# A transformer block in split fp32 on one Trainium2 core: side work of the second span's projections placed elsewhere

## Chip, cores and metric

The kernel runs on one core of one Trainium2 chip. The metric is the device time of one execution in microseconds. The kernel before takes 2897.58 us (median of three runs, 2896.61 to 2900.97).

## What is computed

One layer over 2048 tokens of width 1024, all in fp32 (the reference, cut):

```python
xn = rms_norm(x, mix_norm_g)
proj = xn @ w_in                       # q k v | mq mk mv mo | i f | ga gm
A = chunk_band_attention(q, k, v)      # 8 heads of 64, own chunk of 64 and 8 before it
M = mlstm_chunkwise(conv_silu(mq), conv_silu(mk), mv, i, f)   # 4 heads of 128
M = sigmoid(mo) * headwise_rms_norm(M) * mh_norm_g
y = sigmoid(ga) * (A @ w_att_proj) + sigmoid(gm) * (M @ w_mlstm_proj)
x = x + y @ w_out
x = x + relu(rms_norm(x) @ w_up)**2 @ w_down      # 4096 wide
return rms_norm(x, final_norm_g)
```

## The kernel before

**Blocks and spans.** The tokens are four blocks of 512; blocks 0 and 1 are the first span, 2 and 3 the second ("far"). The first span's projections are plain products, block by block (`dense`, first loop). Everything behind them works on a span at once.

**Split products.** Each fp32 operand is split in two parts that TensorE takes at full rate (a rounded copy by ScalarE, the rest by VectorE: L420 and L422 for a weight tile, L953 and L958 or L955 and L960 for an operand tile). A product is three matmuls: high-high, high-low, low-high.

**Quads.** Most products of the spans use seven products of sums in place of eight (Strassen's scheme in Winograd's form). A quad (`quad`, L564) takes seven weight tiles and seven sets of four operand tiles and issues 7 x 2 x 4 x 3 = 168 matmuls of 512 columns. Its seven products share six banks of PSUM (`PLACES`): a product whose bank was used before waits until that bank was copied (L1742, on ScalarE) or added up (L1750, on VectorE; L1987 in the output projection). `combine` holds these two for all quads but the output projection. The operands' sums are made by `take_parts` (loads L1706, a gain L1709, sums L1719, splits) or by `spread` (L1804 to L1813); a set of five buffers holds them meanwhile.

**Sums of weights.** A quad's weight tiles are sums of four quarter tiles. Either `quad_w` makes them when the quad's turn comes (loads L397, VectorE L439) and, if the second span uses them again, stores them (L434); or `sum_w` makes them ahead (loads L384, VectorE L389, stores to `wsum`), and the loader later fetches seven finished tiles (L402). `sum_w` works in two halves; in each its fourth subtraction waits until the store of the first has landed, since it overwrites that buffer.

**Order of the work.** From 661 us on (all times by the profile of before) stand: two gate quads "gm" of the first span, two output quads (745), then the second span's projections in the order `IN_ORDER`: gm0, gm1, q, mq, vm0, ga0, k, vm1, mk, ga1, mo (mo at 1227); then eight up quads (from 1273), seven passes of the down projection (`down`, with `add_down`, L2187, adding up its banks), and the same from the output projection on for the second span (from 2184). In the first down projection run also attention and recurrence of blocks 2 and 3 (`attention_far`, `recurrence_far`; narrow matmuls L1210, L1245, L1276, L1586 to L1588), and inside it, at two fixed places, each of these blocks' mixer outputs are projected (`project`), for which their attention and recurrence must be done.

**Normalisation of the second span.** `norm_far` loads blocks 2 and 3 twice (L874, L897), squares them (L876), scales them (L899) and stores them as `xn`, from which `take_xn` makes the operands of `IN_ORDER`.

**Who sets the order.** The kernel is written as threads that a planner (`Flow`) runs when the program is built. Each thread asks for an engine with a duration; the planner keeps a clock for each engine, takes the request that can start first, and among those that could start at the same time the one with the lower rank, then the older. The order so found is the order of each engine's instructions in the program; on the chip each engine takes its own in that order and waits where data is late. The durations are the planner's own (`act_ns`, `dve_ns`, 0.67 us for the POOL operation in `after_in`, 2 us from a DMA's issue to its landing). All DMAs are issued by SP, in order, so that one that waits holds those behind it. Pools of buffers (16 `ctx`, 6 `tmp`) make a thread wait as well.

The lines that the prediction speaks of are these: L1742 and L1750 (`combine`), L1987 (`after_out`), L2187 (`add_down`), L1919 (the gate scale of mo, on POOL), L1941 (the convolution's activation, on ScalarE), L1706, L1709 and L1719 (`take_parts`), L389 (`sum_w`), L439 and L434 (`quad_w`).

Of the kernel before, what the change touches and what calls it, by code (L numbers as in the profile page):

```python
# [49 lines left out]
Q_VM, Q_IN = N_Q, dict(q=N_Q + 2, mq=N_Q + 3, ga0=N_Q + 4, k=N_Q + 5, mk=N_Q + 6, ga1=N_Q + 7, mo=N_Q + 8)  # L50
IN_ORDER = ("gm0", "gm1", "q", "mq", "vm0", "ga0", "k", "vm1", "mk", "ga1", "mo")
N_REC = 1
D_SUMS = (3, 6, 9, 11, 12, 13, 14, 15)
PROJ = {2: (4,0), 3: (6,2)}

ORDER = (0, 1, 3, 2, 5, 4, 6)
# [35 lines left out]
class Flow:  # L92
# [77 lines left out]
    def run(self):  # L170
        while self.ready or self.blocked:
            moved = True
            while moved:
                moved = False
                for th in sorted(self.blocked, key=lambda x: (x.prio, x.n)):
                    ok, value = self._grant(th)
                    if ok:
                        self.blocked.remove(th)
                        self.now = th.at
                        self._step(th, value)  # L180
                        moved = True
            if not self.ready and not self.blocked:
                break
            if not self.ready:
                raise RuntimeError("no thread can go on")
            best = None
            for th in self.ready:
                t, frm = th.at
                for e in th.req[0].split("|"):
                    start = t + self.LAT[frm].get(e, 0.0)  # L190
                    if e == "pe" and th.prio < 5:
                        start += self.SLACK
                    key = (max(self.clock[e], start), th.prio, th.n)
                    if best is None or key < best[0]:
                        best = (key, th, e)
            (start, _, _), th, e = best
            self.ready.remove(th)
            end = start + th.req[1]
            self.clock[e] = end
            if len(th.req) > 2:  # L200
                end += th.req[2]
            th.at = self.now = (end, e)
            self._step(th, e)
# [15 lines left out]
class Layer:  # L219
# [98 lines left out]
    def weights(self):  # L318


        part = lambda q, m: ("part", (q, m))
        for b in range(2):
            yield from (("plain", n) for n in range(N_W))
        yield from (part(q, m) for q in range(N_G + N_O) for m in range(7))
        for name in IN_ORDER:
            if name[:2] == "vm":
                yield from (part(Q_VM + kk, m) for m in range(7) for kk in range(2))
            elif name[:2] == "gm":
                yield from (part(int(name[2]), m) for m in range(7))
            else:  # L330
                yield "quad", (Q_IN[name], False)
        for s in range(NS):
            if s == 1:
                yield from (part(q, m) for q in range(N_G, N_G + N_O) for m in range(7))
            for q in range(N_G + N_O, N_G + N_O + N_F):
                if s == 0:
                    yield "quad", (q, True)
                else:
                    yield from (part(q, m) for m in range(7))
            for p, m in enumerate(ORDER):  # L340
                for q in range(N_Q - N_F, N_Q):
                    if s == 0 and (p, (q - N_Q + N_F) / 2) in PROJ.values():
                        yield from (("plain", N_W - 8 + 4 * x + j) for j in range(4) for x in range(2))
                    yield part(q, m)
# [280 lines left out]
    def dense(self):  # L625
        fl = self.fl
        none = [None] * KT
        for b in range(2):
            B = self.blk[b]
            self.banks.want = 4  # L630
            yield "wait", [B["xs_ev"]]
            fl.spawn(self.attention(b), 1)
            fl.spawn(self.recurrence(b), 1)
            xs = B["xs"]
            vs = xs if b > 0 else B["xg"]
            yield from self.token_tiles(vs, B["xn"], lambda t, bk: self.evac_v(b, t, bk))

            yield "wait", [self.ev_late]
            (bk,) = yield "get", self.banks, 1
            for k in range(KT):  # L640
                yield "pe", 433
                for j in range(2):
                    self.nc.tensor.matmul(bk[:40], self.gw[:, k], vs[k][:, j],
                                          start=k == 0 and j == 0, stop=k == KT - 1 and j == 1)
            fl.spawn(self.gates(b, bk), 1)
            yield from self.token_tiles(vs, none, lambda t, bk: self.evac_mv(b, t, bk))
            self.banks.want = 2
            if b == 0:
                fl.put(self.rpool, *vs)
            for j in range(4):  # L650
                for fn in (self.evac_q, self.evac_k, self.evac_conv_q, self.evac_conv_k, self.evac_og):
                    (bk,) = yield from self.feature_tile(xs, none if b > 0 or j > 0 else B["xs_done"])
                    fl.spawn(fn(b, j, bk), 1)
            if b == 0:
                fl.spawn(self.norm_in(1), 3)
                fl.spawn(self.norm_far(), 3)
            for j in range(8):
                (bk,) = yield from self.feature_tile(xs, none)
                fl.spawn(self.evac_ga(b, j, bk), 1)
            fl.put(self.rpool, *xs)  # L660
            fl.set(B["xs_free"])
            if b == 1:
                G = self.operands()
                for k in range(4):
                    fl.spawn(self.take_xn(0, k, *G), 2)
            early = range(N_G + N_O) if b == 0 else range(Q_VM, Q_VM + 2)
            for q in early:
                fl.spawn(self.sum_w(q), 3)
            self.banks.want = 3
            for x, evac in ((0, self.evac_att), (1, self.evac_rec)):  # L670
                for j in range(4):
                    yield "wait", B["mix_ev"][4 * x:4 * x + 4]
                    bks = yield from self.pair_tile(B["mix"][4 * x:4 * x + 4], none)
                    for n in range(2):
                        fl.spawn(evac(b, 2 * j + n, bks[n]), 1)
                fl.put(self.rpool, *B["mix"][4 * x:4 * x + 4])
# [11 lines left out]
            yield from self.quad(*O, self.after_out(0, i, None), release=i == N_O - 1)  # L688

        for i, name in enumerate(IN_ORDER):  # L690
            if i in D_SUMS:
                fl.spawn(self.sum_w(N_Q - N_F + D_SUMS.index(i)), 3)
            last = name == IN_ORDER[-1]
            if last:
                for k in range(4):
                    fl.spawn(self.take_x2(k, *U), 2)
            if i == 1:
                yield from self.gates_in(*X)
            if name[:2] == "vm":
                yield from self.quad_tok(int(name[2]), *X, self.after_vm(int(name[2])))  # L700
            else:
                yield from self.quad(*X, self.after_in(name), release=last)
        for s in range(NS):
# [4 lines left out]
                        fl.spawn(self.take(self.hd.ap(), self.h_ev, 1.0, (0, 1), *U), 2)  # L708
                    yield from self.quad(*O, self.after_out(1, i, U), release=i == N_O - 1)
            for i in range(N_F):  # L710
                if s == 0 and len(IN_ORDER) + i in D_SUMS:
                    fl.spawn(self.sum_w(N_Q - N_F + D_SUMS.index(len(IN_ORDER) + i)), 3)
                if i == 2:
                    for h in range(2):
                        fl.spawn(self.norm_mid(s, h), 3)
# [981 lines left out]
    def take_parts(self, src, kept, scale, k, A, aev, g=None):  # L1697
        fl, V = self.fl, self.nc.vector
        if k > 1:
            yield "wait", [aev[m][k - 2] for m in range(7)]  # L1700
        got = yield "get", self.ctx, 5
        a11, a12, a21, a22, s1 = (x[:, :512] for x in got)
        for b, j, a in ((0, k, a11), (0, 4 + k, a12), (1, k, a21), (1, 4 + k, a22)):
            yield "wait", [kept[b][j]]
# [15 lines left out]
            fl.spawn(self.take_split(dst, m, k, A, aev, scale), 1)  # L1720
            done.append(aev[m][k])
        yield "wait", done
        fl.put(self.ctx, *got)

    def take_split(self, src, m, k, A, aev, scale=1.0):
        (r,) = yield "get", self.rpool, 1
# [4 lines left out]
    def combine(self, finish, o=0):  # L1731
# [6 lines left out]
        def copied(n, name, ps, clear):  # L1738
            (t,) = yield "get", self.ctx, 1
            held[n][name] = t  # L1740
            yield "act", act_ns(512, True)
            nc.scalar.copy(t[:, o:o + 512], ps)  # L1742
            fl.set(clear)
            fl.set(ev[n][name])
# [1 line left out]
        def summed(n, name, to, ps, clear):  # L1746
            yield "wait", [ev[n][name]]
            t = held[n][name]
            yield "dve", dve_ns(512)
            nc.vector.tensor_add(t[:, o:o + 512], ps, t[:, o:o + 512])  # L1750
            if clear is None:
                fl.put(self.banks, ps)
# [146 lines left out]
    def after_in(self, name):  # L1899
        fl, nc = self.fl, self.nc  # L1900

        def finish(n, which, t, ps):
# [12 lines left out]
            if ps is not None:  # L1915
                fl.put(self.banks, ps)
            if name == "mo":
                yield "pool", 670
                nc.gpsimd.tensor_scalar(t5, t5, 1.0, self.ghead[:, j:j + 1], op0=ALU.add, op1=ALU.mult)  # L1919
                dst, ev = self.mfar[b].ap()[2 * MH + j], self.m_ev[b, 2 * MH + j]  # L1920
            else:
                x, j = name[:2] == "gm", 4 * hi + 2 * int(name[2]) + n
# [33 lines left out]
    def after_out(self, s, q, U):  # L1956
# [24 lines left out]
        def add(n, w, done, ps, clear):  # L1981
# [1 line left out]
            if done and w != "a21":  # L1983
                yield "wait", [first[n][w]]
            t = xt[n][w][:, :512]
            yield "dve", dve_ns(512)
            V.tensor_add(t, ps, t)  # L1987
            if clear is None:
                fl.put(self.banks, ps)
# [175 lines left out]
    def add_down(self, s, m, j, ps):  # L2165
# [9 lines left out]
        else:  # L2175
# [7 lines left out]
            for to, frm in steps:  # L2183
                if to not in acc:
                    (acc[to],) = yield "get", self.ctx, 1
                yield "dve", dve_ns(512)
                V.tensor_add(acc[to][:, :512], ps, acc[frm][:, :512])  # L2187
                if (m, to) in ((1, lo), (5, far), (5, t), (4, mid)):
                    fl.set(ready[to])
# [126 lines left out]
    def build(self):  # L2316
# [17 lines left out]
        self.wi = 0  # L2334
        self.wtile = {}
        self.wev, self.wgot = collections.defaultdict(Event), collections.defaultdict(Event)
        self.td_ev = {q: E(2) for q in (*range(N_G + N_O), *range(N_Q - N_F, N_Q + 2))}
        self.t_ev = [[E(4) for _ in range(7)] for _ in range(NS)]
        self.xn_kept = [E(KT) for _ in range(NB)]
        self.x_sent, self.w_sent = E(KT), E(KT // 2)  # L2340
# [110 lines left out]
```

## Time and profile before

| | |
|---|---|
| median of three runs | 2897.58 us |
| the profiled execution | 2903.79 us |
| its span, first to last instruction | 2901.7 us |
| mean granted clock of TensorE | 0.993 |
| TensorE matmuls | 2827.3 us busy, 97% |
| VectorE, ScalarE, POOL | 2035.9, 1549.2 and 67.6 us busy |
| DMA | 629.87 MB, 217 GB/s in the mean |

The span is the time between the first and the last instruction; the execution has 2.1 us around it. The busy time of an engine is an average over stages with different limits. TensorE's matmuls are pipelined, so that a matmul of 391 ns follows the one ahead of it sooner than that. How many there are in a stretch, and how long TensorE stands between them, tells more than the busy share. "PEclk" is the share of TensorE's full clock that was granted. A row of waits names who waited, for whom, how long in total, how often, and the longest. In a row of instructions there stand the busy time and mean duration, and behind the second bar the idle time of the engine just ahead of them and what ended it.

### The profile page before, as it was taken

The page shows a single profiled execution, that of the slowest core. Times are in us where ns is not written, and L with a number is a line of the kernel's source. Part 1 is how long each engine was busy: PE and PEld are TensorE (multiplying, and loading weights), DVE is VectorE, ACT ScalarE, POOL GpSimd, SP SyncE. Part 2 cuts the span into 40 slices and gives each one's busy share as a digit, 9 for nine tenths or more (in the row PEclk, how much of TensorE's full clock was granted, in tenths as well). Part 3 has the DMA queues.
Part 4 walks back from the last instruction along what each step waited for, and adds up shares of the span by engine and source line. Part 5 has one row for each costly group of instructions (what it writes and reads, how often), then busy time and mean ns, then how long its engine had stood idle before and what let it go on. Part 6 is the DMA issues. An engine that isn't in the chain of part 4 may idle for free.

```text
span 2901.7 us, 39144 instructions
## 1 busy us (share of the span) xinstructions
PE 2827.3 (97%) x13576; PEld 2351.1 (81%) x13576; DVE 2035.9 (70%) x3778; ACT 1549.2 (53%) x2690; POOL 67.6 (2%) x124
## 2 busy tenths in 40 slices
PE   8999999999999999999999999999899999999998
PEld 7888878887787888877888888788778888888887
DVE  6886579867884865876666787769877744455565
ACT  4665356644453544565555575446645755554444
POOL 0000000000000000020000000000000000000000
PEclk9999999999999999999999999999999999999999
DMA  6328963368974566668877966688468855576563
GB/s 214 99 94 296 318 204 95 103 229 301 306 240 139 200 217 218 203 218 293 291 273 257 272 205 189 200 243 273 147 212 293 270 193 186 188 255 201 192 220 136
DMA packets 287238, 629.87 MB, mean 217 GB/s; under 512 B 31936, under 2 KB 46400, under 8 KB 287040
## 3 DMA queue, kind: packets, MB, share of 16 engines
q1 hardware_dynamic: 287040, 627.38, 65.4%
q8 instruction: 106, 1.74, 0.2%
q14 instruction: 92, 0.75, 0.1%
HBM read 437.46 MB, written 189.79 MB: 216 GB/s over the span
## 4 chain that ended last, share of the span: by engine, by line
PE 75%; DVE 10%; DMA 7%; ACT 4%; issue 3%; POOL 1%; SPq 0%; POOLq 0%; DVEq 0%; ACTq 0%
PE bank L564 33%; PE bank L481 11%; PE bank L482 11%; PE bank L483 11%; PE bank L592 2%; DVE wsp L422 2%; PE bank L1210 2%; PE bank L1245 1%; PE bank L1276 1%; DVE r L958 1%; DMA r<-u 1%; ACT wsp L420 1%; DMA wsum<-ctx 1%; DVE sc L1251 1%; DMA tmp<-in_x 1%
## 5 line engine op out<-in xcount | busy, mean ns | idle before, releaser
L564 PE MATMUL bank<-r,wsp 128*128 128x512 f32 x5208 | 1197.6, 391 | 22.0 <-DVE ctx L1750 9.6
L564 PEld LDWEIGHTS bank<-r,wsp 128*128 128x128 f32 x5208 | 979.7, 189 | 234.2 <-DVE ctx L1750 11.9
L422 DVE TENSOR_TENSOR wsp<-wraw,wsp 128x1024 fp32r<-128x1024 f32 x461 | 563.2, 1222 | 359.5 <-ACT wsp L420 349.2
L420 ACT CAST wsp<-wraw 128x1024 fp32r<-128x1024 f32 x461 | 484.0, 1050 | 526.7 <-PE bank L482 220.7
L481 PE MATMUL bank<-r,wsp 128*128 128x512 f32 x1600 | 640.0, 400 | 1.5 <-DVE scs L1251 0.8
L482 PE MATMUL bank<-r,wsp 128*128 128x512 f32 x1600 | 625.6, 391 | 0.0
L483 PE MATMUL bank<-r,wsp 128*128 128x512 f32 x1600 | 625.5, 391 | 0.0
L483 PEld LDWEIGHTS bank<-r,wsp 128*128 128x128 f32 x1600 | 300.7, 188 | 64.9
L481 PEld LDWEIGHTS bank<-r,wsp 128*128 128x128 f32 x1600 | 301.5, 188 | 54.3 <-DVE tmp L1222 1.2
L482 PEld LDWEIGHTS bank<-r,wsp 128*128 128x128 f32 x1600 | 301.8, 189 | 52.4 <-DVE r L958 0.2
L1750 DVE TENSOR_TENSOR ctx<-bank,ctx 128x512 f32<-128x512 f32 x174 | 118.6, 686 | 91.9 <-PE bank L564 90.3
L953 ACT CAST r<-r 128x512 fp32r<-128x512 f32 x224 | 136.6, 622 | 76.0 <-DMA r<-u 63.1
L958 DVE TENSOR_TENSOR r<-r 128x512 fp32r<-128x512 f32 x224 | 149.3, 687 | 36.5 <-ACT r L953 35.5
L1742 ACT COPY ctx<-bank 128x512 f32<-128x512 f32 x174 | 101.1, 582 | 68.1 <-PE bank L564 63.9
L1260 ACT ACTIVATE sc<-sc,scs 128x640 f32<-128x640 f32 (+4 forms) x128 | 97.4, 761 | 69.8 <-DVE scs L1257 68.5
L389 DVE TENSOR_TENSOR ctx<-ctx,ctx 128x512 f32<-128x512 f32 x112 | 76.4, 689 | 66.5 <-DMA ctx<-in_wf 37.9
L1210 PE MATMUL bank<-r,r 128*128 128x256 f32 (+1 forms) x672 | 111.1, 284 | 6.8 <-DVE r L1281 6.2
L2121 ACT ACTIVATE ctx<-ctx 128x512 f32<-128x512 f32 x96 | 60.6, 631 | 102.6 <-DVE ctx L1750 102.5
L1210 PEld LDWEIGHTS bank<-r,r 128*128 128x128 f32 x672 | 98.7, 191 | 20.2 <-DVE r L1281 9.9
L1251 DVE CUSTOM_DVE_ANT_0 sc<-bank,bias 128x320 f32<-128x320 f32 (+3 forms) x240 | 105.6, 459 | 7.8 <-PE bank L1245 6.8
L1281 DVE TENSOR_TENSOR r<-bank,r 128x512 fp32r<-128x512 f32 (+1 forms) x168 | 96.3, 593 | 10.4 <-ACT r L1279 9.7
L953 ACT CAST r<-ctx 128x512 fp32r<-128x512 f32 x116 | 69.5, 618 | 61.2 <-DMA ctx<-xn 30.2
(274 smaller groups left out, 2906.1 us busy)
## 6 DMA issues: line engine op xcount, KB each, us to landing
wraw<-in_wf SPq DMA_DIRECT2D x168, 512.0 KB, 4.2
wraw<-wsum SPq DMA_DIRECT2D x144, 512.0 KB, 4.1
r<-u SPq DMA_DIRECT2D x224, 256.0 KB, 4.2
wraw<-in_w SPq DMA_DIRECT2D x104, 512.0 KB, 3.8
u<-ctx SPq DMA_DIRECT2D x128, 256.0 KB, 2.7
ctx<-in_wf SPq DMA_DIRECT2D x112, 256.0 KB, 4.5
wsum<-ctx SPq DMA_DIRECT2D x112, 256.0 KB, 3.7
u<-tmp SPq DMA_DIRECT2D x96, 256.0 KB, 3.2
```

Source lines behind the costliest of these rows:

```text
L420: nc.scalar.copy(w[:, 0], raw)
L422: nc.vector.tensor_sub(w[:, 1], raw, w[:, 0].bitcast(F32))
L481: mm(ps, lh, rh, start=first, stop=False)
L482: mm(ps, lh, rl, start=False, stop=False)
L483: mm(ps, ll, rh, start=False, stop=last)
L564: mm(ps, wv[:, x, k, n], a[:, y], start=new and k == 0 and x == y == 0, stop=k == 3 and x == 1, skip_group_check=True)
L953: self.nc.scalar.copy(dst[:, 0], src)
L958: self.nc.vector.tensor_sub(dst[:, 1], src, dst[:, 0].bitcast(F32))
L1210: nc.tensor.matmul(bk[:, c0:c0 + w], st, sl[:, x, o:o + w], start=n == 0, stop=n == total - 1)
L1251: nc.vector.tensor_tensor_reduce(out=e[:, x * w:x * w + w], in0=bks[x][:, :w], in1=br[:, j0 + x * w:j0 + x * w + w], op0=ALU.add, op1=ALU. ...
L1742: nc.scalar.copy(t[:, o:o + 512], ps)
L1750: nc.vector.tensor_add(t[:, o:o + 512], ps, t[:, o:o + 512])
```

## The change

Five things are changed; the computation stays the same.

1. **Rank.** A request for an engine that ends in "!" gets rank -1, ahead of everything. It is used for the operations that free a bank: the copies L1742, the additions L1750, L1987 and L2187.
2. **Sums of weights.** The first two up quads get their sums from `sum_w` too (`N_USUM`), and are then fetched as finished tiles in both spans. The sums of the two "vm" weights, which were made at the end of block 1, now run beside entries 1 and 2 of `IN_ORDER` (counted from 0), the two new ones beside entries 4 and 5, and those of the eight down quads beside entries 7, 9 and 11 to 16 instead of 3, 6, 9 and 11 to 15 (entries from 11 on are up quads).
3. **Normalisation.** `norm_far` starts with block 1's gate tiles instead of block 0's.
4. **Gate scale.** In mo, (t + 1) g is computed by ScalarE as t g + g instead of by POOL.
5. **Buffers of `take_parts`.** Where the scale is 1, every second set is taken from `tmp` instead of `ctx`.

```diff
-D_SUMS = (3, 6, 9, 11, 12, 13, 14, 15)
+N_USUM = 2
+EARLY_SUMS = {1: Q_VM, 2: Q_VM + 1, 4: N_G + N_O, 5: N_G + N_O + 1}
+EARLY_SUMS.update({i: N_Q - N_F + n for n, i in enumerate((7, 9, 11, 12, 13, 14, 15, 16))})
...
                 for e in th.req[0].split("|"):
+                    prio = th.prio
+                    if e[-1] == "!":
+                        e, prio = e[:-1], -1
...
-                    key = (max(self.clock[e], start), th.prio, th.n)
+                    key = (max(self.clock[e], start), prio, th.n)
...
-                if s == 0:
+                if s == 0 and q >= N_G + N_O + N_USUM:
                     yield "quad", (q, True)
...
             if b == 0:
                 fl.spawn(self.norm_in(1), 3)
+            else:
                 fl.spawn(self.norm_far(), 3)
...
-            early = range(N_G + N_O) if b == 0 else range(Q_VM, Q_VM + 2)
-            for q in early:
+            for q in range(N_G + N_O if b == 0 else 0):
                 fl.spawn(self.sum_w(q), 3)
...
-            if i in D_SUMS:
-                fl.spawn(self.sum_w(N_Q - N_F + D_SUMS.index(i)), 3)
+            if i in EARLY_SUMS:
+                fl.spawn(self.sum_w(EARLY_SUMS[i]), 3)
...
-        got = yield "get", self.ctx, 5
+        pool = (self.ctx, self.temp)[k % 2 if scale == 1.0 else 0]
+        got = yield "get", pool, 5
...
-            yield "act", act_ns(512, True)
+            yield "act!", act_ns(512, True)
             nc.scalar.copy(t[:, o:o + 512], ps)
...
-            yield "dve", dve_ns(512)
+            yield "dve!", dve_ns(512)
             nc.vector.tensor_add(t[:, o:o + 512], ps, t[:, o:o + 512])
...
-                yield "pool", 670
-                nc.gpsimd.tensor_scalar(t5, t5, 1.0, self.ghead[:, j:j + 1], op0=ALU.add, op1=ALU.mult)
+                yield "act", act_ns(512, False, 2)
+                g = self.ghead[:, j:j + 1]
+                nc.scalar.activation(t5, t5, AF.Identity, scale=g, bias=g)
```

L1987 and L2187 get the same "dve!" as L1750. All line numbers are those of the kernel before.

More of the change, by code (lines that the diff above doesn't have):

```diff
@@ L710, in dense @@
             for i in range(N_F):
-                if s == 0 and len(IN_ORDER) + i in D_SUMS:
-                    fl.spawn(self.sum_w(N_Q - N_F + D_SUMS.index(len(IN_ORDER) + i)), 3)
+                if s == 0 and len(IN_ORDER) + i in EARLY_SUMS:
+                    fl.spawn(self.sum_w(EARLY_SUMS[len(IN_ORDER) + i]), 3)
                 if i == 2:
@@ L1722, in take_parts @@
         yield "wait", done
-        fl.put(self.ctx, *got)
+        fl.put(pool, *got)
     def take_split(self, src, m, k, A, aev, scale=1.0):
@@ L1985, in add @@
             t = xt[n][w][:, :512]
-            yield "dve", dve_ns(512)
+            yield "dve!", dve_ns(512)
             V.tensor_add(t, ps, t)
@@ L2185, in add_down @@
                     (acc[to],) = yield "get", self.ctx, 1
-                yield "dve", dve_ns(512)
+                yield "dve!", dve_ns(512)
                 V.tensor_add(acc[to][:, :512], ps, acc[frm][:, :512])
@@ L2336, in build @@
         self.wev, self.wgot = collections.defaultdict(Event), collections.defaultdict(Event)
-        self.td_ev = {q: E(2) for q in (*range(N_G + N_O), *range(N_Q - N_F, N_Q + 2))}
+        self.td_ev = {q: E(2) for q in (*range(N_G + N_O + N_USUM), *range(N_Q - N_F, N_Q + 2))}
         self.t_ev = [[E(4) for _ in range(7)] for _ in range(NS)]
```

## The prediction

> **What bounds the kernel now.** I read the page first, then busy time by stretch, then TensorE's waits, then the queues behind the longest wait.
>
> ```profile
> span 2901.7 us, 39144 instructions
> PE 2827.3 (97%) x13576; PEld 2351.1 (81%) x13576; DVE 2035.9 (70%) x3778; ACT 1549.2 (53%) x2690; POOL 67.6 (2%) x124
> L564 PE MATMUL bank<-r,wsp 128*128 128x512 f32 x5208 | 1197.6, 391 | 22.0 <-DVE ctx L1750 9.6
> ```
>
> TensorE is the bound, and the change leaves every matmul in place. Only time in which TensorE stands still, or runs slowly after standing still, can be won. The stretches show where that time is:
>
> ```profile
> core 0: us, PE busy (x) PEld busy (x) DVE busy (x) ACT busy (x) POOL busy (x), PEclk, DMA share, GB/s
> 920.80:958.90 38.10, 38.10 (x170) 31.55 (x169) 21.83 (x28) 15.26 (x21) 0.00 (x0) 1.00 0.47 163
> 661.00:707.00 46.00, 41.63 (x171) 32.16 (x171) 33.34 (x49) 22.66 (x36) 0.00 (x0) 0.96 0.83 291
> 745.40:793.40 48.00, 41.75 (x169) 32.56 (x168) 42.60 (x63) 19.74 (x30) 0.00 (x0) 0.93 0.93 311
> 1226.90:1273.20 46.30, 40.03 (x169) 32.66 (x168) 37.47 (x50) 33.50 (x55) 15.69 (x7) 0.93 0.52 176
> 1273.20:1316.30 43.10, 40.04 (x170) 32.61 (x170) 32.26 (x42) 21.65 (x33) 1.75 (x1) 0.96 0.80 282
> 1845.00:1865.00 20.00, 16.87 (x90) 13.86 (x90) 17.41 (x51) 10.23 (x22) 1.30 (x3) 0.91 0.50 163
> 2062.00:2117.00 55.00, 41.30 (x286) 35.49 (x284) 44.96 (x136) 36.68 (x99) 3.56 (x5) 0.97 0.39 125
> ```
>
> An undisturbed quad of 168 wide matmuls takes 38.1 us (first row). Four quads take longer: the first gate quad (661) by 46.0 - 38.1 = 7.9 us, the first output quad (745) by 9.9, "mo" (1227) by 8.2, the first up quad (1273) by 5.0; together 31.0. The last two rows lie in the first down stage, where attention and recurrence of the far blocks must end before their projection. In those four quads TensorE waits for:
>
> ```profile
> PE bank L564 <- DVE ctx L1750: 9.6, 3, 6.3
> PE bank L564 <- DVE r L960: 3.5, 2, 3.3
> PE bank L564 <- ACT r L953: 2.8, 2, 2.0
> PE bank L564 <- ACT r L955: 2.3, 3, 0.9
> ```
>
> These are either additions that free a bank (L1750) or operand splits. A gap costs more than its length:
>
> ```profile
> 665.00:669.00 4.00, 3.77 (x10) 2.91 (x10) 1.49 (x2) 1.46 (x3) 0.00 (x0) 0.57 0.85 321
> 1306.00:1309.10 3.10, 0.05 (x1) 0.00 (x0) 3.06 (x5) 1.27 (x3) 0.00 (x0) 1.00 0.78 293
> 1309.10:1312.50 3.40, 3.39 (x11) 2.71 (x12) 3.40 (x5) 3.23 (x5) 0.00 (x0) 0.71 0.96 375
> 1312.50:1316.00 3.50, 3.50 (x14) 2.83 (x13) 1.92 (x4) 1.44 (x3) 0.00 (x0) 0.79 0.81 310
> ```
>
> After the gap at 1306 the granted clock is 0.71 and 0.79: 3.4 x 0.29 + 3.5 x 0.21 = 1.7 us more, so that gap costs 3.1 + 1.7 = 4.8. The Trainium skill (TensorE: Matmul & The Clock Gate, "HAM oscillation") has the clock halved only by idle gaps above about 3.4 us. By that rule this gap would cost 3.1 and the sum below would be some 1.7 us smaller; the trace differs, since the clock fell after a gap of 3.06.
>
> **The change, part by part.**
>
> *Gate scale.* Eight POOL operations in "mo" become ScalarE activations.
>
> ```profile
> L1919 POOL TENSOR_SCALAR ctx<-ctx,ghead 128x512 f32<-128x512 f32 x8 | 17.4, 2180 | 669.4 <-ACT ctx L1914 669.4
> SPq L2026 <- POOL ctx L1919: 14.6, 7, 5.5
> 1242.48 0.33 SPq L397 DMA_DIRECT2D wraw<-in_wf  x1
> 1248.32 0.32 SPq L2026 DMA_DIRECT2D mfar<-ctx  x1
> 1248.73 1.97 SPq L1706 DMA_DIRECT2D ctx<-x  x3
> 1251.27 5.04 DMA ctx<-x
> L1941 ACT ACTIVATE ctx<-ctx,cvw 128x512 f32<-128x512 f32 x16 | 12.9, 815 | 10.8 <-DVE ctx L1750 10.8
> L1709 ACT ACTIVATE ctx<-ctx,gcol 128x512 f32<-128x512 f32 x9 | 6.3, 718 | 5.2 <-DMA ctx<-x 5.2
> ```
>
> The planner allows 0.67 us for the POOL operation; it took 2.18. SP, in order, stood from 1242.8 to 1248.3 for a store of its result, and behind that store stood the loads of x2 (L1706). The chain of waits runs from such a load (1251.27) over L1709 and L1719 to the L1750 for which TensorE stood 6.3 us. Loads 5.5 us earlier leave 0.8 of the gap and no half clock (1.7): 8.2 - 7.2 = 1.0 is left. L1941 has the form of the new activation: 815 ns alone; with L1709's 718 in a row, 8 x 0.72 = 5.8. ScalarE's 33.5 us become 39.3 in a quad of 38.1: 1.2 over. I keep 2.2: **-6.0** (bounds 0 and -8.2). Behind the new activation wait only its own stores and ScalarE's next weight split.
>
> *Bank-freeing additions first.* The rank decides only between operations that the planner holds ready together. The order of the instructions as built shows what it did: of the 174 additions of L1750, those with three or more other VectorE operations between the end of their matmuls and themselves fall from 6 to 1 (longest 21 to 11); of the 56 of the down stage (L2187), from 10 to 1. In the first gate quad it goes together with the operand loads: 7 of 16 loads of xn stood inside that quad before and none does now, since half of the sets are taken from the other pool. (Such a set now waits for five of the six tmp buffers, which normalisation and recurrence use too; on SP the loads behind it would wait along. I see no sign of it in the order.) Its L953 wait goes, L1742 is late next; with the DMA share at 0.83 I keep 1.9 of 7.9: **-6.0** (0 to -7.9). In the first output quad the stretch of 20 us around its third product holds 36 instead of 41 VectorE operations:
>
> ```profile
> L1750 DVE TENSOR_TENSOR ctx<-bank,ctx 128x512 f32<-128x512 f32 x174 | 118.6, 686 | 91.9 <-PE bank L564 90.3
> L389 DVE TENSOR_TENSOR ctx<-ctx,ctx 128x512 f32<-128x512 f32 x112 | 76.4, 689 | 66.5 <-DMA ctx<-in_wf 37.9
> L439 DVE TENSOR_TENSOR wraw<-wraw,wraw 128x1024 f32<-128x1024 f32 x60 | 73.9, 1233 | 3.9 <-DMA wsum<-wraw 1.9 <-DMA wraw<-in_wf 1.3
> ```
>
> 5 x 0.69 = **-3.5**; the rest of that wait is the chain from the last gate product to its operand, which no edit shortens (0 to -9.9).
>
> *Sums.* Two more up quads have their sums made early: 16 more L389 (16 x 0.69 = 11.0 us) for 8 fewer L439 (8 x 1.23 = 9.9), and 16 loads and 16 stores more for 8 and 8 fewer of twice the size. VectorE has room in that part (21.83 of 38.10 above), so this hides; without that room it is 1.1 us. But a sum can hold VectorE:
>
> ```profile
> 1297.93 0.69 DVE L1750 TENSOR_TENSOR ctx<-bank,ctx 128x512 f32<-128x512 f32 x1 [0.64 <-PE bank L564]
> 1304.05 1.42 DVE L389 TENSOR_TENSOR ctx<-ctx,ctx 128x512 f32<-128x512 f32 x2 [5.43 <-DMA wsum<-ctx]
> 1305.38 0.68 DVE L1750 TENSOR_TENSOR ctx<-bank,ctx 128x512 f32<-128x512 f32 x1
> wsum<-ctx SPq DMA_DIRECT2D x112, 256.0 KB, 3.7
> ```
>
> Here L389 waited for its own store, which the planner takes at 2 us and which lands in 3.7 at the median; VectorE stood 5.4 us with an L1750 behind, and TensorE stood. In the first two up quads the stores of L434 (512 KB) are gone, so this one place mends: **-3.5** of 5.0 (0 to -5.0). From the first "gm" of the second span on, 24 halves of sums run instead of 16, and one of the 16 cost 4.8: 8/16 x 4.8 = **+2.4** (0 to +10). The Trainium skill (DMA: Bandwidth & Descriptors, "Anatomy of one DMA") gives 2.0 us and the transfer, some 2.6 for this size as an estimate; by that, no half would wait and the sum would be 2.4 better. The trace's 3.7 speaks against it.
>
> *Normalisation.* 32 loads, 16 squares, 16 scalings and 16 stores move from the end of the first block's projections to the second block's; both places are full of narrow work, and the order there has about as much narrow TensorE work without wide matmuls beside it (469 against 445 in runs of twelve or more). **0** (-4 to +4): its cover is the 38 us quads behind, as its result is first read at the second output quad.
>
> *The down stage.* The planner's order shifts there too, though nothing is edited but the rank of L2187. Before, 234 narrow matmuls stood in one run without wide ones (2062 to 2117).
>
> ```profile
> 2063.92 1.05 PE L2266 MATMUL bank<-ones,wraw 128*128 128x2 f32 x8
> 2071.98 1.26 PE L2291 MATMUL bank<-const,ctx 128*128 128x128 f32 x10
> L482 PE MATMUL bank<-r,wsp 128*128 128x512 f32 x10 | 4.4, 436 | 0.0
> ```
>
> Two more of them take 1.26 - 1.05 = 0.21 us, so undisturbed ones follow each other in 0.11. 286 x 0.11 = 31.5 of 55 us: 23.5 lost. In the new order the runs there have 34 and 48: 82/234 x 23.5 = 8.2, **-15.3** (-5 to -20). But the run ahead of the other block's projection grows from 46 to 106. In 1845 to 1865, 30 wide (L482's ten and as many of each of its neighbours; 38.1/168 = 0.227 each) and 60 narrow need 13.4 of 20: 6.6 lost. 106 by the rate of the long run (0.10 each) lose 10.6, by that of the short one (0.143) 15.2: +4.0 or +8.6, between them **+6.0** (0 to +10).
>
> Sum: -6.0 - 6.0 - 3.5 - 3.5 + 2.4 + 0 - 15.3 + 6.0 = **-25.9 us**. The profiled execution took 2903.8 us (span 2901.7 and 2.1 around it), 6.2 above the median of 2897.6. 2903.8 - 25.9 = 2877.9; from the median, **2872 us**.
>
> **Rivals.**
> (A) All four quads run clean and the down stage gives its better bound: -31.0 + 2.4 - 15.3 + 4.0 = -40, 2858 us. For it: nearly all late additions are gone from the order. Against: VectorE at 42.6 of 48 in the output quad.
> (B) The additions were late because of data, not rank, and the down stage only moves its stall from one block's end to the other's: -6.0 - 3.5 + 2.4 - 5 + 8.6 = -3.5, 2894 us. For it: the wait in "mo" began at a load, and VectorE was busy only 45 of 55 us in the long run, so chains bound part of it.
> (C) Slower: halves of sums hold VectorE while a bank's addition stands behind.
>
> ```profile
> DVE ctx L389 <- DMA wsum<-ctx: 17.1, 11, 5.4
> ```
>
> Eleven such waits stand between 640 and 1600 us, one of them 5.4. Each that reaches TensorE costs 4.8; beyond the 2.4 above, six eat the gain (28.3/4.8), eight make it slower by over 0.2%, ten of the 24 give 2917 us. For it: more sums, more stores. Against: TensorE has three waits on L1750 there, and only one goes back to L389.
> (D) The change does not do what it says, the rank deciding nothing on the chip: only the gate scale counts, 2892 us.
>
> **Chances.** Forecast 0.64; A 0.12; B 0.11; C 0.10; D 0.03. A measurement of this kernel can tell about 0.2% (5.8 us) from no change. Faster: the forecast, A and a little of B and D, 0.78; within 0.2%: 0.12; slower: C, 0.10. The range leaves out A's better end and C: 2853 to 2893.
>
> **What would show it.** "mo" and the first up quad at 38 to 41 us; no SP wait on POOL in "mo"; L1750 gone from the top of TensorE's waits for L564; the first gate quad under 41 and the first output quad still above 42; in the first down stage, TensorE's idle time before narrow matmuls moved in part from the second far block's end to the first's and smaller in sum. The forecast is wrong if VectorE stands for L389 longer than 17 us in that part and L1750 stays, or if TensorE's idle time ahead of the first far block's projection is above 20 us.

## The result and the profile after

The changed kernel takes 2883.05 us (median of 4 runs, 2876.25 to 2886.3) against 2898.64 for the kernel before on the same chip. The ratio is 0.9943, with an interval of 0.9922 to 0.9964: 15.6 us faster. The forecast was 25.9 us and 2872; the range 2853 to 2893 holds the time.

From here on line numbers are those of the changed kernel where a row of it is shown: L570 is the quad's matmul (L564 before), L1749 and L1757 are the bank's copy and addition (L1742, L1750), L882 and L905 the squares and scalings of `norm_far` (L876, L899), L395 the sums (L389), L1927 the gate scale, L959 with L964 and L961 with L966 the operand splits (L953 with L958, L955 with L960), L426 and L428 the weight split. The other kernels' lines differ by one or two from these. First the page of the changed kernel:

```profile
span 2884.5 us, 39213 instructions
PE 2823.1 (98%) x13576; PEld 2352.4 (82%) x13576; DVE 2033.1 (70%) x3783; ACT 1558.3 (54%) x2701; POOL 48.2 (2%) x116
L570 PE MATMUL bank<-r,wsp 128*128 128x512 f32 x5208 | 1199.4, 392 | 17.7 <-DVE ctx L1757 9.9
```

TensorE's work is the same and its wait for the bank additions is still there, 9.9 us after 9.6. The busy time by stretch, for the same quads as before (two gate quads, first output quad, gm0 of the second span with its small gate matmuls, mo) and for the two runs of narrow matmuls in the first down stage:

```profile
core 0: us, PE busy (x) PEld busy (x) DVE busy (x) ACT busy (x) POOL busy (x), PEclk, DMA share, GB/s
648.50:692.80 44.30, 40.22 (x169) 32.42 (x168) 23.64 (x31) 20.95 (x36) 0.00 (x0) 0.96 0.83 281
692.80:737.00 44.20, 41.15 (x169) 33.47 (x168) 35.73 (x51) 25.67 (x44) 0.00 (x0) 0.92 0.94 314
737.00:780.90 43.90, 40.56 (x177) 31.82 (x176) 35.84 (x53) 16.41 (x23) 1.01 (x1) 1.00 0.87 293
819.80:872.40 52.60, 50.66 (x218) 38.00 (x218) 40.75 (x70) 25.50 (x40) 0.00 (x0) 0.97 0.79 272
1217.60:1256.70 39.10, 38.39 (x169) 31.46 (x169) 34.41 (x49) 34.28 (x58) 0.00 (x0) 1.00 0.57 193
1836.00:1864.00 28.00, 22.69 (x126) 19.75 (x125) 22.66 (x70) 15.16 (x36) 1.31 (x3) 0.88 0.51 153
2080.00:2098.00 18.00, 13.26 (x72) 10.81 (x71) 13.43 (x28) 13.61 (x35) 0.00 (x0) 0.81 0.59 209
```

mo went from 46.3 to 39.1 us. But the second gate quad, undisturbed before, is now at 44.2. The following table has the stretches between the first matmuls of the quads, in us, from one profiled execution each:

| stretch | before | after | forecast | after - before |
|---|---|---|---|---|
| start to first gate quad | 661.0 | 648.5 | 0 | -12.5 |
| gate quads | 84.3 | 88.6 | -6.0 | +4.3 |
| first output quad | 48.0 | 43.9 | -3.5 | -4.1 |
| gm0 with gates | 48.5 | 52.5 | 0 | +4.0 |
| mo | 46.4 | 39.1 | -6.0 | -7.3 |
| first up quad | 43.0 | 41.4 | -3.5 | -1.6 |
| last up quad and down stage | 635.6 | 632.2 | -9.3 | -3.4 |
| first output quad, second span | 43.6 | 47.8 | 0 | +4.2 |
| all the rest | 1291.3 | 1290.5 | +2.4 | -0.8 |
| span | 2901.7 | 2884.5 | -25.9 | -17.2 |

TensorE's waits from 650 to 1330 us:

```profile
PE bank L570 <- DVE ctx L1757: 8.3, 5, 3.1
PE bank L570 <- ACT r L961: 2.6, 1, 2.6
PE bank L570 <- ACT ctx L1749: 2.3, 1, 2.3
PE bank L570 <- DVE r L964: 1.9, 1, 1.9
```

The long wait of 6.3 is gone, and several of 2 to 3 us have come. One of them stands in the first gate quad. On ScalarE:

```profile
671.38 0.63 ACT L882 ACTIVATE tmp<-tmp 128x512 f32<-128x512 f32 x1 [4.86 <-DMA tmp<-in_x]
671.91 0.19 ACT L882 ACTIVATION_READ_ACCUMULATOR tmp<-tmp 128x1 f32 x1
672.00 0.57 ACT L1749 COPY ctx<-bank 128x512 f32<-128x512 f32 x1
```

and on TensorE:

```profile
667.72 2.65 PE L570 MATMUL bank<-r,wsp 128*128 128x512 f32 x11
672.62 1.66 PE L570 MATMUL bank<-r,wsp 128*128 128x512 f32 x4 [2.25 <-ACT ctx L1749]
```

ScalarE stood 4.9 us for a load of the moved normalisation, with a bank's copy behind it; the copy done, TensorE went on. From 640 to 800 us this was ScalarE's longest wait in sum:

```profile
ACT tmp L882 <- DMA tmp<-in_x: 19.9, 8, 4.9
ACT wsp L426 <- PE bank L570: 19.0, 8, 4.4
```

### The profile page after: what moved, and what is told of

Same layout as the page of the kernel before. It is cut to its first block, busy times and chain, and to the rows that moved or that the text cites. A ratio compares the mean times of both kernels' runs of the same rounds, so it can differ in the third digit from the quotient of the medians.

```text
span 2884.5 us, 39213 instructions
## 1 busy us (share of the span) xinstructions
PE 2823.1 (98%) x13576; PEld 2352.4 (82%) x13576; DVE 2033.1 (70%) x3783; ACT 1558.3 (54%) x2701; POOL 48.2 (2%) x116
## 4 chain that ended last, share of the span: by engine, by line
PE 72%; DVE 11%; DMA 10%; ACT 3%; issue 2%; SPq 1%; POOL 0%; DVEq 0%; POOLq 0%; ACTq 0%
PE bank L570 32%; PE bank L487 10%; PE bank L488 10%; PE bank L489 10%; PE bank L598 2%; DVE wsp L428 2%; PE bank L1216 2%; DMA r<-u 2%; PE bank L1282 1%; PE bank L1251 1%; DMA proj<-tmp 1%; DMA wsum<-ctx 1%; DVE r L964 1%; DMA ctx<-in_wf 1%; DVE sc L1257 1%
## 5 line engine op out<-in xcount | busy, mean ns | idle before, releaser
L570 PE MATMUL bank<-r,wsp 128*128 128x512 f32 x5208 | 1199.4, 392 | 17.7 <-DVE ctx L1757 9.9
L570 PEld LDWEIGHTS bank<-r,wsp 128*128 128x128 f32 x5208 | 981.4, 189 | 229.1 <-DVE ctx L1757 12.8
L428 DVE TENSOR_TENSOR wsp<-wraw,wsp 128x1024 fp32r<-128x1024 f32 x461 | 563.6, 1223 | 328.9 <-ACT wsp L426 298.9
L426 ACT CAST wsp<-wraw 128x1024 fp32r<-128x1024 f32 x461 | 484.3, 1050 | 493.1 <-PE bank L570 195.3
L959 ACT CAST r<-r 128x512 fp32r<-128x512 f32 x224 | 136.1, 622 | 78.2 <-DMA r<-u 73.2
L1757 DVE TENSOR_TENSOR ctx<-bank,ctx 128x512 f32<-128x512 f32 x174 | 119.2, 688 | 83.4 <-PE bank L570 82.5
L964 DVE TENSOR_TENSOR r<-r 128x512 fp32r<-128x512 f32 x224 | 149.8, 688 | 35.6 <-ACT r L959 34.6
L395 DVE TENSOR_TENSOR ctx<-ctx,ctx 128x512 f32<-128x512 f32 x128 | 87.5, 689 | 94.5 <-DMA ctx<-in_wf 73.7
L1749 ACT COPY ctx<-bank 128x512 f32<-128x512 f32 x174 | 101.0, 582 | 63.9 <-PE bank L570 57.0
L1257 DVE CUSTOM_DVE_ANT_0 sc<-bank,bias 128x320 f32<-128x320 f32 (+3 forms) x240 | 105.4, 460 | 13.7 <-PE bank L1251 12.1
L1285 ACT CAST r<-bank 128x512 fp32r<-128x512 f32 (+1 forms) x168 | 81.8, 516 | 21.2 <-PE bank L1282 17.0
```

The lines of the kernel that those rows point to most:

```text
L426: nc.scalar.copy(w[:, 0], raw)
L428: nc.vector.tensor_sub(w[:, 1], raw, w[:, 0].bitcast(F32))
L570: mm(ps, wv[:, x, k, n], a[:, y], start=new and k == 0 and x == y == 0, stop=k == 3 and x == 1, skip_group_check=True)
L959: self.nc.scalar.copy(dst[:, 0], src)
L964: self.nc.vector.tensor_sub(dst[:, 1], src, dst[:, 0].bitcast(F32))
L1257: nc.vector.tensor_tensor_reduce(out=e[:, x * w:x * w + w], in0=bks[x][:, :w], in1=br[:, j0 + x * w:j0 + x * w + w], op0=ALU.add, op1=ALU. ...
```

## The experiments

**Theory** after the result: work in the background that stands in an engine's queue ahead of a bank's copy or addition, and waits for a load, is what the early quads pay for. So the moved normalisation gives time ahead of the first gate quad and takes more in the quads behind it, and something else in the change must give the gain. **Rivals**: the rank gives it; the normalisation is worth nothing, as forecast; the DMA load alone makes these quads long. The ratios are to the kernel before, timed beside each of them, with 95% intervals; they compare better than the medians, which come from different sessions.

| kernel | median us | ratio to before | interval |
|---|---|---|---|
| after | 2883.05 | 0.9943 | 0.9922 to 0.9964 |
| e1 after, normalisation back | 2876.93 | 0.9916 | 0.9900 to 0.9932 |
| e2 after, no rank | 2880.57 | 0.9928 | 0.9913 to 0.9942 |
| e3 after, gate scale on POOL | 2882.95 | 0.9939 | 0.9917 to 0.9961 |
| e4 after, all sums back | 2898.49 | 0.9992 | 0.9981 to 1.0004 |
| e5 after, sets in ctx only | 2887.49 | 0.9948 | 0.9933 to 0.9962 |
| e6 before + gate scale | 2889.57 | 0.9957 | 0.9941 to 0.9973 |
| e7 before + normalisation moved | 2905.18 | 1.0009 | 0.9999 to 1.0019 |
| e8 after, normalisation earlier | 2885.89 | 0.9941 | 0.9926 to 0.9955 |
| e9 before + vm sums moved | 2891.39 | 0.9969 | 0.9956 to 0.9981 |
| e10 before + vm sums + gate scale | 2881.52 | 0.9935 | 0.9914 to 0.9956 |
| e11 after, normalisation back, no rank | 2878.10 | 0.9915 | 0.9899 to 0.9931 |
| e12 after, only the vm sums moved | 2883.01 | 0.9940 | 0.9920 to 0.9960 |

**e1, the normalisation back in the first block.**

```diff
-            else:
                 fl.spawn(self.norm_far(), 3)
```

> After, with the normalisation of the second span started in the first block again. Theory (the move gives time ahead of the first gate quad and takes it back in the gate quads, where ScalarE stands for its loads with bank copies behind): the first gate quad starts some 10 us later than in after, the two gate quads and gm0 together are 10 to 15 us shorter, the whole is within 6 us of after (2877 to 2889). Rival (the move is worth nothing, as predicted; the gate quads are long for another reason): start and gate quads as in after, both within 3 us.

The gate quads and the first output quad of this kernel:

```profile
656.50:694.60 38.10, 38.10 (x169) 31.53 (x169) 23.35 (x31) 17.57 (x26) 0.00 (x0) 1.00 0.83 281
694.60:732.70 38.10, 38.10 (x170) 31.53 (x168) 32.91 (x48) 23.45 (x36) 0.00 (x0) 1.00 0.90 316
732.70:772.60 39.90, 38.51 (x169) 31.38 (x168) 35.54 (x53) 15.23 (x23) 0.00 (x0) 1.00 0.95 328
```

The first gate quad starts 8.0 us later (656.5), and these three and gm0 take 166.0 us after 185.0: 19 us less. Both gate quads are undisturbed, at a DMA share of 0.83 to 0.95, so the DMA load alone does not make them long. 0.9916 against 0.9943 speaks for the normalisation's place costing some 8 us net (the intervals overlap a little). The rival "worth nothing" is wrong in both halves: the move gave 8 and took 19.

**e2, no rank.**

```diff
-                        e, prio = e[:-1], -1
+                        e = e[:-1]
```

> After, with the rank of bank-freeing operations taken away. Theory (the rank is worth 3 to 8 us, mainly in the gate quads and the first down stage): 2886 to 2891. Rival 1 (the rank carries the whole gain): 2895 or more. Rival 2 (late data, not rank, sets those waits): within 3 us of after.

0.9928: the change does as well without the rank. Theory and rival 1 fall, and the time is that of rival 2. In the order of this kernel as built (counted there, not in a trace), 5 additions of L1757 and 12 of the down stage again have three or more operations ahead of them (1 and 1 in after). They cost nothing that can be measured; its first gate quad is longer than in after (47.6), the second undisturbed (38.1).

**e3, the gate scale on POOL again.**

```diff
-                yield "act", act_ns(512, False, 2)
-                g = self.ghead[:, j:j + 1]
-                nc.scalar.activation(t5, t5, AF.Identity, scale=g, bias=g)
+                yield "pool", 670
+                nc.gpsimd.tensor_scalar(t5, t5, 1.0, self.ghead[:, j:j + 1], op0=ALU.add, op1=ALU.mult)
```

> After, with the gate scale of mo on POOL again. Theory (SP stands behind POOL, loads of x2 come late): mo takes 44 to 47 us instead of 39, the whole 2888 to 2891, and SP's wait for POOL is back in mo. Rival (the rank alone mended mo): mo at 39 to 41, the whole as after.

The time and mo are the rival's, but SP stands for POOL again (L2033 is the store, L1926 the POOL operation):

```profile
SPq L2033 <- POOL ctx L1926: 13.6, 7, 3.3
```

Yet mo takes 39.7 us and the whole is as after. So SP's standing for POOL does not by itself make mo long. Which of the other four edits keeps it short here is not shown; e5 speaks for the buffers.

**e5, all operand sets in ctx.**

```diff
-        pool = (self.ctx, self.temp)[k % 2 if scale == 1.0 else 0]
+        pool = self.ctx
```

> After, with every operand set of take_parts in ctx. Theory (loads of the first gate quad and of x2 come later): first gate quad or mo 1 to 5 us longer, the whole 2884 to 2889. Rival (the pool does not matter): within 2 us of after.

mo at 44.5 us, with ScalarE waiting for x2 loads, the longest 3.3 us:

```profile
1217.20:1261.70 44.50, 41.06 (x170) 33.39 (x169) 33.31 (x47) 36.63 (x60) 0.00 (x0) 0.92 0.55 186
```

The whole, 2887.49 us, is where the theory had it, but 0.9948 cannot be told from after.

**e6, the gate scale alone on the kernel before** (the diff of e3 the other way round).

> Before, with the gate scale on ScalarE and nothing else. Theory: mo falls from 46 to 39 or 40 us, the whole 2890 to 2893 (6 to 8 us under before). Rival (ScalarE becomes the bound of mo, or the rank is needed too): mo at 43 or more, the whole above 2894.

mo at 39.7 us, with ScalarE busy 35.3 of it; 0.9957, 12 us. In the kernel before this one edit mends mo. mo shows 6.7 of them. The first up quad behind it shows 4.8 more: it takes 38.2 us after 43.0, though the sums of its weights are made as before. VectorE's 5.4 us wait for a store of sums, to which the prediction put that quad's loss, is gone. (Of the kernels made from before, those with POOL take 86.9 to 89.4 us for these two quads together, e6 and e10 with ScalarE 77.9 and 78.5.) One caution: the order ahead of mo is that of before, and yet the first gate quad started at 655.9 instead of 661.0, so 5 us between two executions can be mere spread.

**e4, all sums at their old places.**

```diff
-N_USUM = 2
+N_USUM = 0
...
-            for q in range(N_G + N_O if b == 0 else 0):
+            early = range(N_G + N_O) if b == 0 else range(Q_VM, Q_VM + 2)
+            for q in early:
```

> After, with the sums of weights at their old places. Theory (24 halves instead of 16 cost little, the first up quad gains little): within 4 us of after. Rival (more sums hold VectorE): 4 us or more faster than after. Second rival (the sums taken away from the end of block 1 are what brought the first gate quad forward): it starts 5 us or more later than in after.

The whole gain is gone, 0.9992. That is neither the theory nor a rival: the first gate quad starts as in after (646.6), but is then 50.8 us long, and the first output quad 52.5:

```profile
646.60:697.40 50.80, 41.64 (x169) 32.72 (x169) 33.47 (x47) 20.87 (x32) 0.00 (x0) 0.90 0.91 307
737.40:789.90 52.50, 45.01 (x178) 34.82 (x177) 42.34 (x64) 21.21 (x34) 1.01 (x1) 0.90 0.90 305
```

How the sums do it shows in the first gate quad. In this kernel L394 is the subtraction of `sum_w`, L1757 the bank's addition:

```profile
685.41 0.69 DVE L394 TENSOR_TENSOR ctx<-ctx,ctx 128x512 f32<-128x512 f32 x1 [6.11 <-DMA wsum<-ctx]
689.69 2.92 PE L569 MATMUL bank<-r,wsp 128*128 128x512 f32 x6 [7.62 <-DVE ctx L1757]
```

VectorE stood 6.1 us until a store of the vm sums had landed, with two bank additions behind (686.62 and 688.95); TensorE stood 7.6 us for the second. It is the mechanism of rival C, at a place that the prediction did not look at.

**e9, the vm sums alone moved, on the kernel before.**

```diff
-            early = range(N_G + N_O) if b == 0 else range(Q_VM, Q_VM + 2)
-            for q in early:
+            for q in range(N_G + N_O if b == 0 else 0):
...
+EARLY_SUMS = {1: Q_VM, 2: Q_VM + 1}
```

> Before, with the sums of the two vm weights moved from the end of block 1 to entries 1 and 2 of the second span's projections, and nothing else. Theory (with these sums back the whole gain was gone, so their place carries most of it): the two gate quads at 38 to 40 us each and the first output quad at 40 to 43, together 12 to 20 us under before; mo stays at 46; the whole 2881 to 2888. Rival (the sums of the first two up quads carry it, or the sums only take away what the moved normalisation costs): gate and output quads as in before, the whole within 5 us of before.

Gate quads 38.1 and 39.0, output quad 42.0: 13 us less than before. In before, ScalarE stood for loads of xn in the first gate quad (650 to 700 us):

```profile
ACT r L953 <- DMA ctx<-xn: 13.5, 2, 6.8
```

In e9 this wait is gone from the same 50 us; why the loads landed so late beside the sums was not followed. gm0 gives 7.7 back (56.2 after 48.5). VectorE's longest wait from 825 to 880 us (L2065 adds up the squares of another normalisation, the one ahead of the up quads) and TensorE's only one there (L1750 is the bank's addition in this kernel):

```profile
DVE bias L2065 <- ACT sc L2061: 6.3, 1, 6.3
```

```profile
PE bank L565 <- DVE ctx L1750: 5.4, 1, 5.4
```

VectorE stood with a bank's addition behind it, and TensorE 5.4 us for that. Mo stays at 48.2. 0.9969, 9 us; less than expected, and not the rival's.

**e12, after with only the vm sums moved** (`N_USUM = 0`, the down quads' sums at 3, 6, 9, 11 to 15).

> After, without the sums of the first two up quads, and those of the down quads at their old places; the vm sums stay moved. Theory (the vm sums carry what the sums' move gives): within 5 us of after (2878 to 2888). Rival (the up quads' sums carry it): 2893 or more.

As after: the sums of the up quads and the down quads' new places are worth nothing measurable. And e12 differs from e4 in the place of the vm sums alone: 0.9940 against 0.9992, so with the normalisation moved this place is worth 15 us.

**e7, the normalisation alone moved, on the kernel before.**

> Before, with the normalisation moved to the second block and nothing else. Theory: the first gate quad starts 8 to 13 us earlier, the gate quads and gm0 give 8 to 14 back: 2893 to 2901. Rival (the earlier start comes from the sums or the pool): the first gate quad starts within 4 us of before.

The first gate quad starts at 645.7, 15.3 us earlier (up to 5 of it may be spread, see e6); it is then 56.2 us long, and the first output quad 52.3. 1.0009: nothing, or a little slower. This and e1 show both halves of the move, with and without the vm sums beside it. In this gate quad TensorE stood in its own queue for the normalisation itself, whose small matmuls (L888) need the sums of the squares:

```profile
667.06 2.07 PE L888 MATMUL bank<-const,r_x 128*128 128x128 f32 x8 [7.79 <-POOL r_x L884]
```

**e8, the normalisation started ahead of block 1's twenty feature tiles.**

> After, with the normalisation started ahead of block 1's twenty feature tiles instead of behind them, so that it ends before the gate quads. Theory (its squares in the gate quads hold ScalarE): the gate quads and gm0 together 8 to 14 us shorter, some of it lost ahead of them; 2868 to 2878. Rival (DMA at over 0.9 in the gate quads, not the squares, makes them long): the gate quads as in after, the whole at 2883 or more.

The rival's number, but not its reason (e1 had as much DMA). The squares now end at 617 us, ahead of the gate quads, but the scalings run until 718, and hold VectorE instead. VectorE's waits for their loads from 645 to 800 us, and TensorE's two longest from 649 to 835:

```profile
DVE tmp L905 <- DMA tmp<-in_xt: 12.1, 6, 5.7
```

```profile
PE bank L570 <- DVE ctx L1757: 6.3, 2, 5.8
PE bank L570 <- ACT r L961: 5.3, 2, 4.4
```

The 5.8 us fit: VectorE stood 5.7 us for a scaling's load until 680.8, with three bank additions behind; TensorE went on at 688.0, after the third. The 4.4 us (756) lie behind the last scaling and have another cause, not followed. So "its squares on ScalarE" was too narrow: its scalings hold VectorE in the same way.

**e10, vm sums and gate scale on the kernel before.**

> Before, with the vm sums moved and the gate scale on ScalarE, and nothing else. Theory (these two are the gain, the other three edits cost or do nothing): both savings, mo at 38 to 40 besides; 2872 to 2880, below after. Rival (the rank or the tmp sets are needed): above 2883.

0.9935: 19 us, about what e6 (12) and e9 (9) give together, and no less than all five edits. The expected further gain over after isn't there.

**e11, after with the normalisation back and no rank.**

> After, with the normalisation back in the first block and the rank taken away. Theory (the first is worth some 7 us, the rank nothing): 2872 to 2880. Rival (the rank is needed where the gate quads are clean): 2883 or more.

0.9915, the same as e1: the rank is not needed there either. e1 and e11 are the best kernels found, 22 to 24 us under before.

## Why the prediction was right, and where it was not

**Right: the bound.** Time was to be won only where TensorE stands or runs slowly after it: of the 17.2 us of the span, 13.0 are less standing time and 4.2 less busy time for the same matmuls (2827.3 to 2823.1).

**Luck in the number.** The places did not pay as forecast. Ahead of the first gate quad, forecast 0, lie -12.5 us. The five places with a gain forecast, together -28.3, gave -12.1. gm0 and the second span's first output quad, forecast 0, took 8.2. That the sum lies well inside the range is in good part that one miss made up for others. Of the signs named, mo at 39.1, no wait of SP for POOL in mo, the output quad above 42 and the down stage's shift came. The first gate quad under 41 (it took 44.3), the first up quad at 38 to 41 (41.4) and L1750 off the top of TensorE's waits did not.

**Right: mo.** -6.0 forecast, -7.3 measured; e6 shows the edit alone doing it. Wrong inside the term: ScalarE does not become the bound (34.3 us busy of 39.1, where 39.3 was worked out: its 33.5 us belonged to a stretch of 46, not of 38). But e3 shows that with the other four edits POOL may stay; that this is the work of the x2 sets in tmp is likely by e5, and was not tried alone.

**Wrong place: the first up quad.** Its -3.5 was put to the sums made early. But the kernels tried without early sums (e4, e6, e7, e9, e10, e12) have it at 38.1 to 39.0, e7 and e9 behind a mo of 48; those with them at 38.5 to 44.4. In after, sums for the down quads hold it:

```profile
1293.92 0.69 DVE L395 TENSOR_TENSOR ctx<-ctx,ctx 128x512 f32<-128x512 f32 x1 [4.20 <-DMA ctx<-in_wf]
1294.54 0.68 DVE L1757 TENSOR_TENSOR ctx<-bank,ctx 128x512 f32<-128x512 f32 x1
```

TensorE stood 2.5 us for the addition.

**Wrong: "Normalisation, 0".** The term had two large parts. Ahead of the first gate quad the work was not covered (8 us by e1, 15 by e7, with the spread named there); the 38 us quads named as its cover have VectorE and ScalarE time to spare, but no time to stand. A square that waited 4.9 us for its load held a bank's copy, and TensorE stood 2.3 us (after); a scaling that waited 5.7 us held additions, and TensorE stood 5.8 us (e8). I had weighed its busy time, and its first reader, but not what stands behind it in its own engines' queues.

**Wrong by omission: the vm sums.** The sums' term counted the eight halves added later, not those taken from the end of block 1. Their place is worth 9 us alone (e9) and 15 when the normalisation is moved too (e4 against e12). The gate scale alone is worth 12 (e6), and the two together as much as the whole change (e10). The first output quad's -3.5 (measured -4.1) was put down to fewer VectorE operations there; e9 and e1 with 42.0 and 39.9 show that the quad is mostly held by such background work, and not, as the prediction has it, by a chain that no edit shortens.

**Wrong: the rank.** It does change the order (late additions 6 to 1 and 10 to 1), but that is worth nothing that can be measured: e2 has 5 and 12 of them, e11 has 4 of L1757 again, and neither is slower than its partner with the rank. The gate quads' -6.0 did not come (+4.3). Rival D, at 0.03, had the rank right, but not the rest.

**Down stage: the two prices fair, the sum not.** By the prediction's rule (0.227 us for a wide matmul, 0.11 for a narrow one) the run at the second block's end lost 23.5 us and those in its place lose 8.9 (8.2 forecast: 18.0 us, 10 wide, 62 narrow). The run ahead of the first block's projection lost 6.6 and now 10.4 (12.6 forecast: 28.0 us, 32 wide, 94 narrow). Together -10.8. (The prediction scaled by 234 narrow matmuls where its own row has 286 in all, so its 8.2 is a rough figure.) But the stage gained 3.4: about 7 us came back as small losses in stretches that were clean, such as 2.2 at 1940 to 1950 and 2.8 at 1990 to 2010. Spread work was taken to be free work. Nor is the gain the rank's: without it, e2 (runs of 127 and 89 in its order as built) has the stage at 630.7 and e11 at 630.8. All kernels made from after have it at 625.8 to 635.7, all made from before at 635.6 to 640.4; which edit does it is open.

**Rival C came only in small.** VectorE's waits for loads of sums doubled between 640 and 1600 us (20.3 before), those for their stores stayed (17.1 before; the sign of being wrong, over 17 us for L389, can only mean these, and was just missed):

```profile
DVE ctx L395 <- DMA ctx<-in_wf: 45.0, 26, 4.2
DVE ctx L395 <- DMA wsum<-ctx: 16.6, 10, 3.7
```

Stores of sums landed in 4.2 us at the median (3.7 before). Most waits cost little: the quads from gm1 to ga1 take 38.1 to 39.3 us in after. The one of 4.2 us is that of the first up quad above.

**Open.** The stretches are from one execution each and vary by up to 5 us, so only the larger differences carry weight. e1 and e11 lie some 5 us below e10 by the ratios, but the intervals overlap; whether the other edits give anything is not shown. That the first output quad of the second span is 4.2 us longer in after was not tried by itself; in e1 and e2 it is not.

## What to carry to other kernels

Background work is not hidden by an engine's idle share: it is hidden only where nothing urgent stands behind it in the same queue while its load is late, so look for a place where the urgent work can wait, and price a move at both ends. An order that looks better by a count (late additions, uncovered runs) has to be tried alone; here the count fell from 10 to 1, and without the edit that did it the time is the same. When five edits come together, undo each and try the likely ones alone: two of these gain as much alone as all five, and one takes some 8 us back.

## What the runs showed of the hardware

Idle gaps of TensorE of 2 to 3 us were often, but not always, followed by a halved clock. Around the gap of 3.05 us in the second gate quad of after, and, in the last row, over its first up quad:

```profile
725.60:728.70 3.10, 0.05 (x2) 0.03 (x1) 2.77 (x5) 1.63 (x4) 0.00 (x0) 0.85 0.82 301
728.70:732.10 3.40, 3.40 (x8) 2.72 (x9) 3.40 (x6) 3.25 (x5) 0.00 (x0) 0.50 0.92 299
732.10:735.50 3.40, 3.40 (x11) 2.64 (x11) 2.43 (x4) 2.27 (x4) 0.00 (x0) 0.64 0.98 358
1256.70:1298.10 41.40, 38.67 (x169) 31.39 (x168) 24.82 (x35) 23.31 (x37) 0.00 (x0) 1.00 0.87 298
```

The granted clock (0.85, 0.50, 0.64) falls at the end of the gap and stays low behind it. In the two stretches behind it, 3.4 x 0.50 + 3.4 x 0.36 = 2.9 us were lost on top of it, nearly as much as the gap itself. In before, the gap of 2.03 us in the first gate quad (ended by L953) was followed by 0.57 from 665 to 669. But the first output quad of after has a gap of 2.64 us (ended by L961 at 759.3) and the first up quad one of 2.48 (ended by L1757 at 1295.3), and both quads were granted 1.00. So the length of a single gap does not decide it here; what does was not tried.

The POOL operation on 128x512 that the planner takes at 0.67 us took 0.69 to 6.2 us in before (median 1.73); what made it vary was not tried.
